# Expert stage in the order of the source, tokens gathered as float32 from x itself, 20 weight slots, last down-projection in two halves

## The chip, the cores and the metric

The program runs on one core of a Trainium2 chip. A core has five engines that run their own instruction streams and meet at semaphores: TensorE (PE, matrix multiply; its weight loads are listed apart as PEld), VectorE (DVE), ScalarE (ACT), GpSimd (POOL) and SyncE (SP, which here only issues DMAs). The metric is device time of one execution in microseconds (us), lower is better. Before the change the median of three runs is 1189.18 us (1188.09 to 1191.92).

## What is computed

Two transformer blocks on 256 tokens of width 1024, and a final RMS norm. The change lies in the last part of the second block, a mixture of 32 experts in 4 groups; every token goes to its two best experts:

```python
merged = sigmoid(gate_r) * ret_out + sigmoid(gate_d) * diff_out
x = x + g1 * dot(merged, w_out)
h2 = rmsnorm(x, norm_ffn) * (1.0 + sc2) + sh2
y = hierarchical_moe(h2, w_router_group, b_router_group, w_router_expert,
                     b_router_expert, w_exp_gate, w_exp_up, w_exp_down)
    # for a token and each of its two experts e, with the router's weight:
    # dot(silu(dot(h2, w_exp_gate[e])) * dot(h2, w_exp_up[e]), w_exp_down[e])
x = x + g2 * y
return rmsnorm(x, norm_final)
```

Each expert has 1024x512 gate and up matrices and a 512x1024 down matrix, all float32: 192 MB of weights for the stage.

## The kernel before

The stage (`moe`, from L1361) treats 32 experts as 16 pairs j, with 64 slots for tokens to an expert, so that a pair fills the 128 partitions. Its weights come as 192 loads of 1 MB (128 x 2048 floats) on SP's queue, in the order in which `stream` yields them: for each pair 4 loads of gate, 4 of down of the pair before, 4 of up. A load goes into the next of 18 slots in rotation: 4 of pool "early", 3 raw2h, 1 raw2, 2 raw2b, 4 raw, 1 raw2c, 3 spm. A slot's DMA waits until PE has read what lay there. SP is in order, so a DMA that waits holds back all behind it.

What PE does for a pair j, in the source's order:

- `up(j)` for the gate: 32 matmuls of 64 columns of tokens by 512 (L1442), two experts side by side; then tanh on ACT and a product on DVE;
- `down(j-1)`: 32 such matmuls (L1464) into two PSUM banks, which ACT and DVE split into a high and a low part (L1469, L1470);
- `up(j)` again for the up matrix;
- in every odd j but 7 and 15: `gather(j+1)`, which brings the tokens of the next two pairs into `xg` (L1407, 32 records of 128x256); call such a j a turn;
- `scatter(j-1)`: 8 matmuls with the transposed one-hot GT that add to Y, four PSUM banks (L1390, L1391);
- `slots_T(j+1)`: GT for the next pair (L1422, L1424), and `turned`: the hidden layer transposed by four matmuls whose stationary operand is `th[:, f:512:4]`, every fourth float (L1450).

For `gather`, the routing part ahead of the stage makes `xs`, x scaled by its norm and split into high and low halves, each regrouped so that 128 columns lie side by side (L1179 on ACT, L1182 on DVE, both for two token tiles). The gather multiplies `xs` with a one-hot G of the slots (L1398).

At j = 7 the stage drains and branches, for the case that an expert has more than 64 tokens; gather(8) comes right behind the branch. At j = 15 one more slot is taken for `nf` and `g2`, two row vectors that `rows` spreads over the partitions (32 matmul records, L872), and another for `yacc`, the sum of x and the experts. Then come down(14), the last scatter, and the last pair's down-projection in three pieces of columns (L1533 and `piece`), each followed by its product with g2, its own scatter (L1572, L1573, L1575), and its squares. The tail scales by the norm and writes out (L1548 to L1555).

A scheduler orders the instructions of each engine: the source's order is only its input, and matmuls of one helper can be put among those of another.

Of the kernel before, what the change touches and what calls it, by code (L numbers as in the profile page):

```python
# [25 lines left out]
NRAW = 4  # L26
CHECK = 7
NRAW2B = 2
# [4 lines left out]
PIECES = ((0, 512), (512, 256), (768, 256))  # L33
# [58 lines left out]
class Build:  # L92
# [135 lines left out]
    def sq_part(self, ss, x, t, half, n=512):  # L228

        scr = self.t(self.sm, [128, 512], "sqs", bufs=1)  # L230
        row = x[:, t, :] if len(x.shape) == 3 else x
        self.nc.scalar.activation(scr[:, 0:n], row[:, half * n:(half + 1) * n], AF.Square, accum_out=ss[:, t, half:half + 1])
# [39 lines left out]
    def setup(self):  # L272
# [8 lines left out]
        self.sp_ctx = ExitStack()  # L281
        self.sp = self.pool("sp", 3, ctx=self.sp_ctx, side="right")
# [655 lines left out]
    def block2(self, x, ss, inner, outer):  # L938
# [184 lines left out]
        xs = self.xs = [T(self.xtp, [128, 2, 8, 128], "xl", F32R) for _ in range(2)]  # L1123
# [48 lines left out]
        for t in range(2):  # L1172
# [16 lines left out]
    def moe_setup(self):  # L1189
# [11 lines left out]
        for i, v in enumerate((self.a2, self.sh2)):  # L1201
            w = T(p, [128, 8, 16], "spread")
            nc.vector.tensor_mul(w, v[:, :, None].to_broadcast([128, 8, 16]), cm[:, None, 228:244].to_broadcast([128, 8, 16]))
            nc.tensor.matmul(pp[:, i * 8:i * 8 + 8], w.rearrange("p a b -> p (a b)"), cm[:, 244:252], start=True, stop=True)
# [94 lines left out]
    def stream(self):  # L1299
# [29 lines left out]
        def down(j):  # L1329
            w2 = [d["w_exp_down_2"][0, e].rearrange("(p f) c -> p f c", f=4) for e in (2 * j, 2 * j + 1)]  # L1330
            if j < 15:
                for b in range(2):
                    for a in range(2):
                        raw = slot()
                        put(raw, w2[a][:, b * 2:b * 2 + 2, :])
                        yield raw
                return
            for c in range(2):
                raws = [slot() for _ in range(2)]
                for c0, w, i, f, nf in [z for z in LAST if z[0] // 512 == c]:  # L1340
                    if nf * w == 2048:
                        put(raws[i], w2[i][:, :, c0:c0 + w])
                    else:
                        o = raws[i][c0 // 256 % 2][:, f * w:(f + nf) * w]
                        nc.sync.dma_start(o.rearrange("p (f c) -> p f c", f=nf), w2[i][:, f:f + nf, c0:c0 + w])
                yield from raws

        for j in range(16):
            yield from wide("w_exp_gate_2", j)
            if j == 15:  # L1350
                yield slot()
            elif j not in (0, CHECK + 1):
                yield from down(j - 1)
            yield from wide("w_exp_up_2", j)
            if j == 15:
                yield slot()
                yield from down(14)
            if j in (CHECK, 15):
                yield from down(j)

    def moe(self, x, ctx):  # L1361
# [12 lines left out]
        slots += whole(self.raw, "raw", NRAW) + whole(self.raw2c, "raw2c", NRAW2C) + whole(self.sp, "spm", 3)  # L1374
# [18 lines left out]
        def gather(j):  # L1393

            G = []
            for t in range(2):
# [3 lines left out]
                G.append(o)  # L1400
            xg = xgs[0] = xgs[0] or T(self.xtp, [128, 8, 256], "xh")
# [12 lines left out]
            return G, xg  # L1414
# [64 lines left out]
        G, xg = gather(0)  # L1479
        hT = None  # L1480
        for j in range(16):
            pgt = up(j)
            if j == 0:
                self.weights()
                GT, ws = slots_T(0, G)
# [3 lines left out]
            if j == 15:  # L1489
# [3 lines left out]
            elif hT is not None:  # L1493
                down(hT)
            pu = up(j)
            nc.vector.scalar_tensor_tensor(th, th, ws, pu, op0=OP.mult, op1=OP.mult)  # L1496
            GTj = GT
            if j == 15:
                yacc = load()[0:2]
                last = []  # L1500
                down(hT, lambda: last.append(turned(th, p2, "xg")))
                scatter(14, GTp, yp[:, 0], yp[:, 1])
                for t in range(2):
                    for c in range(2):
                        ccs = slice(c * 512, (c + 1) * 512)
                        nc.vector.tensor_mul(yacc[t][:, ccs], Y[t][c], g2[:, ccs])  # L1506
                        nc.gpsimd.tensor_add(yacc[t][:, ccs], yacc[t][:, ccs], x[:, t, ccs])  # L1507
                break
            if j % 2 == 1 and j != CHECK:
                G, xg = gather(j + 1)  # L1510
# [6 lines left out]
            if j == CHECK:  # L1517
                drain(j)
                hT = None
                G, xg = gather(j + 1)  # L1520
                GT, ws = slots_T(j + 1, G)
        hTt = last[0]

        fs = T(p1, [128, 2, 4], "fss")
        yfs = T(self.xtp, [128, 8, 256], "xh").rearrange("p k s -> p (k s)")
        tail = ()
        for q, (c0, n) in enumerate(PIECES):
            if c0 % 512 == 0:
                raws = [load() for _ in range(2)]
            py = self.acc()  # L1530
            for f in range(4):
                for i in range(2):
                    nc.tensor.matmul(py[i * 64:(i + 1) * 64, 0:n], hTt[:, f, i * 64:(i + 1) * 64],  # L1533
                                     raws[i][(c0 // 256 % 2) if n == 256 else f // 2][:, f * n % 1024:f * n % 1024 + n], start=(f == 0), stop=(f == 3))
# [3 lines left out]
            tail = self.piece(q, c0, n, py, GTj, yacc, fs, nf, g2, yfs[:, c0:c0 + n])  # L1538
# [18 lines left out]
    def piece(self, q, c0, n, py, GT, yacc, fs, nf, g2, yf):  # L1557

        nc = self.nc
        T = self.t  # L1560
        cs = slice(c0, c0 + n)
        nc.vector.tensor_mul(yf, py[:, 0:n], g2[:, cs])
        if q == 0:
            yh, yl = T(self.sm, [128, 512], "pf", F32R), T(self.p2, [128, 512], "yl", F32R, 1)
            nc.scalar.copy(yh, yf)
            nc.vector.tensor_sub(yl, yf, yh.bitcast(F32))
        yield
        for t in range(2):
            pc = self.mis()
            g = GT[:, t * 128:(t + 1) * 128]  # L1570
            if q == 0:
                nc.tensor.matmul(pc, g, yh, start=True, stop=False)  # L1572
                nc.tensor.matmul(pc, g, yl, start=False, stop=True)  # L1573
            else:
                nc.tensor.matmul(pc[:, 0:n], g.bitcast(F32), yf, start=True, stop=True)  # L1575
            nc.vector.tensor_add(yacc[t][:, cs], yacc[t][:, cs], pc[:, 0:n])
            scr = T(self.sm, [128, 512], "sqs", bufs=1)
            nc.scalar.activation(scr[:, 0:n], yacc[t][:, cs], AF.Square, accum_out=fs[:, t, q:q + 1])
            if q == 0:
                nc.gpsimd.tensor_mul(yacc[t][:, cs], yacc[t][:, cs], nf[:, cs])  # L1580

    def overflow(self, p1, p2, x, Y):
# [5 lines left out]
        with tc.If(most > 64):  # L1588
            with tc.For_i(0, 32, 1) as e:
                n = nc.values_load(cnt[0:1, bass.ds(e, 1)], min_val=0, max_val=256)  # L1590
                with tc.If(n > 64):
# [5 lines left out]
                    def part(name, k):  # L1597
                        src = d[name][0, bass.ds(e, 1)]
                        src = src.rearrange("o (p f) c -> p (o f) c", f=4) if name == "w_exp_down_2" else src.rearrange("o (p k) c -> p (o k) c", k=8)
                        w = T(self.sm, [128, 512], "sqs", bufs=1)  # L1600
# [6 lines left out]
                    for b in range(1, 4):  # L1607
                        G, Gr = [], []
                        for t in range(2):
# [5 lines left out]
                            o = T(p2, [128, 64], f"Gr{t}", bufs=1)  # L1615
# [4 lines left out]
                        xg = T(p2, [128, 8, 64], "xg", bufs=1)  # L1620
# [107 lines left out]
```

## Time and profile before

| | us |
|---|---|
| median of three runs | 1189.18 |
| the profiled execution | 1188.83 |
| its span in the trace | 1186.9 |
| PE busy in the span | 1131.5 |
| first gate matmul of the expert stage, from the span's start | 723.4 |
| first gate matmul of pair 15 | 1136.6 |

The span is what the trace covers; 1.9 us of the execution lie outside it. A view by windows lists, for each stretch, its length, every engine's busy time with the number of records, the granted clock of PE (1.00 is the full 2.4 GHz level, 0.50 the 1.2 GHz one), the DMA engines' share and the rate. Timeline and chain rows begin with the start and the length of a run of like instructions. A float32 matmul over the full array appears as two records.

### The profile page before, as it was taken

What the parts mean: (1) busy time and instruction counts of PE and PEld (TensorE: products, weight loads), DVE (VectorE), ACT (ScalarE), POOL (GpSimd) and SP (SyncE); (2) the same over time, 40 slices, a digit from 0 to 9 for tenths busy, and PEclk for the clock granted to TensorE, in tenths of its full rate; (3) what the DMA queues carried; (4) which work ended last, traced back from release to release, by engine and by line L of the source; (5) the groups of instructions that cost most, each with busy time, mean ns of one, the idle gap of its engine ahead of it and who ended that gap; (6) DMA issues with size and microseconds to landing.
All of it is one profiled execution on the core that took longest, in us unless ns stands there. A gap on an engine that the chain in (4) does not pass through costs nothing. (4 is left out here: it accounts for less than half of the span.)

```text
span 1186.9 us, 16106 instructions
## 1 busy us (share of the span) xinstructions
PE 1131.5 (95%) x6502; PEld 808.6 (68%) x6503; DVE 550.8 (46%) x862; ACT 393.6 (33%) x679; POOL 188.6 (16%) x137
## 2 busy tenths in 40 slices
PE   7999988999999999999899999999999799999997
PEld 6788766898999798998899975434343344344443
DVE  2767655876666684788565643111111111111103
ACT  2434434555444445434544441111011011110112
POOL 0422531322011130532220210000000000000003
PEclk9999988999999999999999998999999999999999
DMA  8345524687777746657357575999999999999993
GB/s 269 105 144 177 178 87 142 245 279 288 248 283 255 244 142 194 197 162 264 142 152 285 182 281 218 421 421 419 421 421 421 420 420 420 421 421 421 421 415 129
DMA packets 86654, 331.64 MB, mean 279 GB/s; under 512 B 5520, under 2 KB 10272, under 8 KB 62512
## 3 DMA queue, kind: packets, MB, share of 16 engines
q1 hardware_dynamic: 84080, 327.70, 73.1%
q10 hardware_dynamic: 2448, 2.79, 0.8%
q8 instruction: 52, 0.85, 0.3%
q14 instruction: 26, 0.21, 0.0%
q0 software_dynamic: 48, 0.08, 0.0%
HBM read 329.50 MB, written 1.05 MB: 279 GB/s over the span
## 5 line engine op out<-in xcount | busy, mean ns | idle before, releaser
L145 DVE TENSOR_TENSOR lo<-raw,hi 128x1024 fp32r<-128x1024 f32 x156 | 208.0, 1342 | 96.2 <-ACT hi L144 95.8
L144 ACT CAST hi<-raw 128x1024 fp32r<-128x1024 f32 x176 | 183.6, 1047 | 203.2 <-PE acc L169 76.8
L169 PE MATMUL acc<-xl,hi 128*128 128x256 f32 x448 | 127.7, 285 | 0.9 <-DVE xl L958 0.8
L168 PE MATMUL acc<-xh,hi 128*128 128x256 f32 x448 | 128.0, 286 | 0.0
L170 PE MATMUL acc<-xh,lo 128*128 128x256 f32 x448 | 127.3, 284 | 0.0
L169 PEld LDWEIGHTS acc<-xl,hi 128*128 128x128 f32 x448 | 86.4, 193 | 1.4 <-DVE xl L958 1.3
L168 PEld LDWEIGHTS acc<-xh,hi 128*128 128x128 f32 x448 | 86.3, 193 | 0.1
L170 PEld LDWEIGHTS acc<-xh,lo 128*128 128x128 f32 x448 | 86.2, 192 | 0.1
L211 PE MATMUL acc<-hi,xh 128*128 128x512 f32 x208 | 84.2, 405 | 0.0
L212 PE MATMUL acc<-lo,xh 128*128 128x512 f32 x208 | 83.2, 400 | 0.0
L213 PE MATMUL acc<-hi,xl 128*128 128x512 f32 x208 | 82.3, 397 | 0.0
L1442 PE MATMUL mis<-raw,xh 128*64 128x512 f32 x288 | 79.5, 594 | 0.0
L1507 POOL TENSOR_TENSOR raw2h<-raw2h,x 128x512 f32<-128x512 f32 x4 | 5.0, 1280 | 458.1 <-DVE raw2h L1506 458.1
L169 PE MATMUL mis<-xl,hi 128*128 128x256 f32 x256 | 72.6, 284 | 1.4 <-DVE xl L270 1.4
L168 PE MATMUL mis<-xh,hi 128*128 128x256 f32 x256 | 72.7, 284 | 0.0
L170 PE MATMUL mis<-xh,lo 128*128 128x256 f32 x256 | 72.4, 283 | 0.0
L1488 DVE SCALAR_TENSOR_TENSOR pf<-pf,mis 128x512 f32<-128x512 f32 x16 | 11.0, 688 | 123.8 <-ACT pf L1487 123.7
L145 POOL TENSOR_TENSOR lo<-raw,hi 128x1024 fp32r<-128x1024 f32 x20 | 48.4, 2421 | 101.9 <-ACT hi L144 101.9
L1470 DVE TENSOR_TENSOR xh<-mis,xh 128x512 fp32r<-128x512 f32 x30 | 20.8, 692 | 88.4 <-ACT xh L1469 88.2
L856 DVE SCALAR_TENSOR_TENSOR ada<-raw,sc,ada 128x1024 f32<-128x1024 f32 x42 | 56.7, 1350 | 9.1 <-DMA raw<-in_w_ada 8.5
L1442 PE MATMUL mis<-spm,xh 128*64 128x512 f32 x200 | 58.0, 596 | 0.0
L1442 PE MATMUL mis<-raw2h,xh 128*64 128x512 f32 x200 | 57.6, 595 | 0.0
(464 smaller groups left out, 2133.8 us busy)
## 6 DMA issues: line engine op xcount, KB each, us to landing
raw<-in_w_in SPq DMA_DIRECT2D x46, 1024.0 KB, 5.4
raw<-in_w_ff SPq DMA_DIRECT2D x32, 1024.0 KB, 6.0
raw<-in_w_exp_up SPq DMA_DIRECT2D x25, 1024.0 KB, 19.8
raw<-in_w_ada SPq DMA_DIRECT2D x24, 1024.0 KB, 5.7
early<-in_w_exp_down SPq DMA_DIRECT2D x18, 1024.0 KB, 20.1
raw<-in_w_exp_down SPq DMA_DIRECT2D x17, 1024.0 KB, 19.8
raw2h<-in_w_exp_up SPq DMA_DIRECT2D x16, 1024.0 KB, 19.8
spm<-in_w_exp_gate SPq DMA_DIRECT2D x15, 1024.0 KB, 20.1
```

What stands on the lines that cost most here:

```text
L144: nc.scalar.copy(hi, raw)
L145: (nc.gpsimd if self.total in POOL else nc.vector).tensor_sub(lo, raw, hi.bitcast(F32))
L168: nc.tensor.matmul(o, hi[:, w], xh[:, k, :], start=(k == 0 and cb % 2 == 0), stop=False, skip_group_check=True)
L169: nc.tensor.matmul(o, hi[:, w], xl[:, k, :], start=False, stop=False, skip_group_check=True)
L170: nc.tensor.matmul(o, lo[:, w], xh[:, k, :], start=False, stop=(k == 7), skip_group_check=True)
L211: nc.tensor.matmul(o, xh[:, k, ts], hi, start=(k == k0), stop=False)
L212: nc.tensor.matmul(o, xh[:, k, ts], lo, start=False, stop=False)
L213: nc.tensor.matmul(o, xl[:, k, ts], hi, start=False, stop=(k == k1))
L856: nc.vector.scalar_tensor_tensor(a, raw[:, kk, :], self.sc[:, k:k + 1], a, op0=OP.mult, op1=OP.add)
L1442: nc.tensor.matmul(o[i * 64:(i + 1) * 64, :], xg[:, k, j % 2 * 128 + i * 64:j % 2 * 128 + (i + 1) * 64], raws[i][kk // 2][:, kk % 2 * 512: ...
L1470: nc.vector.tensor_sub(yp[:, 1, c, :], py[c], yp[:, 0, c, :].bitcast(F32))
L1488: nc.vector.scalar_tensor_tensor(th, th, 1.0, pgt, op0=OP.add, op1=OP.mult)
```

## The change

In the expert stage PE, DVE and ACT now run in the order of the source (`manual_schedule`); SP and POOL are still ordered by the scheduler. `gather` reads x itself as float32: the stationary operand is `x[:, t, k:1024:8]`, every eighth float, and the moving one is Gr, the one-hot times the norm's factor, made by eight short DVE operations (`scaled`). That is 16 float32 matmuls of 128x256. `xs` and its four operations are gone, and its two buffers ("xl") become slots 19 and 20. G is still made (`onehot`), for `slots_T`.

The order of loads at the end is new: gate 15, up 15, a slot for yacc, `last(0)` (columns 0 to 511 of the last pair's down matrices), down 14, `last(1)` (the other columns, in 5 DMAs). The slot for nf and g2, with its `rows`, moves from j = 15 to j = 13, just ahead of up(13). The first half of the last down-projection runs ahead of down(14) and goes into Y unscaled; the second half comes last in two pieces of 256 columns. POOL now does the second half's additions of x and the products with nf of the first half.

```diff
-            xk = x[:, t, :].rearrange("p (q k) -> p k q", k=8)
-            nc.scalar.mul(xs[0][:, t], xk, r)
...
-            nc.vector.scalar_tensor_tensor(xs[1][:, t], xk, r, xs[0][:, t].bitcast(F32), op0=OP.mult, op1=OP.subtract)
...
         for j in range(16):
             yield from wide("w_exp_gate_2", j)
-            if j == 15:
+            if j not in (0, CHECK + 1, 15):
+                yield from down(j - 1)
+            if j == 13:
                 yield slot()
-            elif j not in (0, CHECK + 1):
-                yield from down(j - 1)
             yield from wide("w_exp_up_2", j)
-            if j == 15:
-                yield slot()
-                yield from down(14)
-            if j in (CHECK, 15):
+            if j == CHECK:
                 yield from down(j)
+        yield slot()
+        yield from last(0)
+        yield from down(14)
+        yield from last(1)
...
+        slots += whole(self.raw, "raw", NRAW) + whole(self.raw2c, "raw2c", NRAW2C) + whole(self.xtp, "xl", 2) + whole(self.sp, "spm", 3)
...
+                    nc.vector.tensor_scalar(Gr[t][:, e * 64:(e + 1) * 64], iota, P[:, t, 2 * j + e:2 * j + e + 1], r3[:, t:t + 1],
+                                            op0=OP.is_equal, op1=OP.mult)
...
-                    for i, (part, t) in enumerate(((0, 0), (0, 1), (1, 0), (1, 1))):
-                        nc.tensor.matmul(ps[:, kk, :], self.xs[part][:, t, k, :], G[t], start=(i == 0), stop=(i == 3))
+                    for t in range(2):
+                        nc.tensor.matmul(ps[:, kk, :], x[:, t, k:1024:8], Gr[t], start=(t == 0), stop=(t == 1))
...
+        self.ordered = ctx.enter_context(self.tc.manual_schedule(engines=ORDERED))
...
+        yacc = load()[0:2]
+        hTt = turned(th, p2, "h15")
+        raws = [load() for _ in range(2)]
...
+        down(hT, first)
+        scatter(14, GTp, yp[:, 0], yp[:, 1])
+        for c in range(2):
+            ccs = slice(c * 512, (c + 1) * 512)
+            for t in range(2):
+                nc.vector.tensor_mul(yacc[t][:, ccs], Y[t][c], g2[:, ccs])
+                (nc.vector if c == 0 else nc.gpsimd).tensor_add(yacc[t][:, ccs], yacc[t][:, ccs], x[:, t, ccs])
...
+            nc.scalar.activation(yfs[:, 1024:1536], yacc[t][:, 0:512], AF.Square, accum_out=fs[:, t, 0:1])
+            nc.gpsimd.tensor_mul(yacc[t][:, 0:512], yacc[t][:, 0:512], nf[:, 0:512])
```

On PE, at the end of pair 4 (no gather there): before, from the last matmul of down on. "mis" are PSUM banks, "acc" the banks of Y, "xh" is xg in the rows of L1442 and the split result of down in those of L1390 and L1391.

```order
L1464 MATMUL mis_7157<-spm_7172,pf_7126 64x512
L1390 MATMUL acc_6546<-xh_6581,GT_6959 128x512
L1390 MATMUL acc_6548<-xh_6581,GT_6959 128x512
L1391 MATMUL acc_6546<-xh_6581,GT_6959 128x512
L1391 MATMUL acc_6548<-xh_6581,GT_6959 128x512
L1390 MATMUL acc_6547<-xh_6581,GT_6959 128x512
L1390 MATMUL acc_6549<-xh_6581,GT_6959 128x512
L1442 MATMUL mis_7186<-spm_7187,xh_6586 64x512
L1391 MATMUL acc_6547<-xh_6581,GT_6959 128x512
L1391 MATMUL acc_6549<-xh_6581,GT_6959 128x512
L1422 MATMUL mis_7220<-ca_84,G_1222_7055 128x128
```

After, at the same place of pair 4, from the last two matmuls of up on (lines L1454, L1389, L1390, L1434 are the old L1442, L1390, L1391, L1422):

```order
L1454 MATMUL mis_7168<-raw2c_7181,xh_6596 64x512
L1454 MATMUL mis_7168<-xl_7183,xh_6596 64x512
L1389 MATMUL acc_6544<-xh_6583,GT_6947 128x512
L1390 MATMUL acc_6544<-xh_6583,GT_6947 128x512
L1389 MATMUL acc_6546<-xh_6583,GT_6947 128x512
L1390 MATMUL acc_6546<-xh_6583,GT_6947 128x512
L1389 MATMUL acc_6545<-xh_6583,GT_6947 128x512
L1390 MATMUL acc_6545<-xh_6583,GT_6947 128x512
L1389 MATMUL acc_6547<-xh_6583,GT_6947 128x512
L1390 MATMUL acc_6547<-xh_6583,GT_6947 128x512
L1434 MATMUL mis_7202<-ca_87,G_1221_7027 128x128
```

The scatter and `slots_T` stood ahead of up, with one matmul of up among them; now all of up is ahead of the scatter.

On SP, the last loads of the stage before, from the last of gate 15 on (two DMAs of a half column range at L1316, then L1345); in brackets are the semaphores waited for, "PE_49" being PE's progress.

```order
L1316 DMA spm_9080<-in_w_exp_gate 128x2048 [waits DMAHW4_49,PE_49]
L1316 DMA early_9119<-in_w_exp_up 128x2048 [waits DMAHW5_49,PE_49]
L1316 DMA early_9121<-in_w_exp_up 128x2048 [waits DMAHW6_49,PE_49]
L1316 DMA early_9131<-in_w_exp_up 128x2048 [waits DMAHW7_49,PE_49]
L1316 DMA raw2h_9133<-in_w_exp_up 128x2048 [waits DMAHW0_49,PE_49]
L1316 DMA raw2h_9147<-in_w_exp_down 128x2048 [waits DMAHW1_49,PE_49]
L1316 DMA raw_1683_9149<-in_w_exp_down 128x2048 [waits DMAHW2_49,PE_49]
L1316 DMA raw2b_9166<-in_w_exp_down 128x2048 [waits DMAHW3_49,PE_49]
L1316 DMA raw2b_9168<-in_w_exp_down 128x2048 [waits DMAHW4_49,PE_49]
```

After, from the last load of gate 15 on:

```order
L1313 DMA early_8976<-in_w_exp_gate 128x2048 [waits DMAHW4_49,PE_49]
L1313 DMA early_8990<-in_w_exp_up 128x2048 [waits DMAHW5_49,PE_49]
L1313 DMA early_8992<-in_w_exp_up 128x2048 [waits DMAHW6_49,PE_49]
L1313 DMA early_9002<-in_w_exp_up 128x2048 [waits DMAHW7_49,DMAHW4_49,PE_49]
L1313 DMA raw2h_9004<-in_w_exp_up 128x2048 [waits DMAHW0_49]
L1313 DMA raw2h_9023<-in_w_exp_down 128x4x512 [waits DMAHW1_49]
L1313 DMA raw_1616_9024<-in_w_exp_down 128x4x512 [waits DMAHW2_49]
L1313 DMA raw2b_9042<-in_w_exp_down 128x2048 [waits DMAHW3_49]
L1313 DMA raw2b_9044<-in_w_exp_down 128x2048
L1313 DMA raw_9058<-in_w_exp_down 128x2048 [waits DMAHW5_49]
L1313 DMA raw_9060<-in_w_exp_down 128x2048 [waits DMAHW6_49]
L1343 DMA raw_9096<-in_w_exp_down 128x4x256 [waits DMAHW7_49]
```

The last load of gate 15 now stands in a buffer of "early". Of the four buffers of that pool one holds nf and g2 from j = 13 to the end, so that the third load of up 15 (early_9002) goes into the buffer in which that last load of gate 15 (early_8976) lies: it waits for that load's landing (DMAHW4) and for PE to have read it. The loads behind it wait for no PE.

## Rows read from the trace of the kernel before

**Rows 1.** The page's first part: busy time, share of the span, records.

```profile
PE 1131.5 (95%) x6502; PEld 808.6 (68%) x6503; DVE 550.8 (46%) x862; ACT 393.6 (33%) x679; POOL 188.6 (16%) x137
```

**Rows 2.** View by windows; pairs 0–14, 1, 2, 4, 5, 7–8, and 15 to the end.

```profile
core 0: us, PE busy (x) PEld busy (x) DVE busy (x) ACT busy (x) POOL busy (x), PEclk, DMA share, GB/s
723.40:1136.62 413.22, 399.38 (x1905) 174.41 (x1904) 66.84 (x135) 56.15 (x103) 0.00 (x0) 0.99 1.00 415
740.26:768.02 27.76, 27.76 (x148) 13.30 (x147) 5.66 (x11) 4.99 (x9) 0.00 (x0) 1.00 1.01 421
768.02:791.94 23.92, 23.92 (x116) 9.46 (x115) 3.82 (x9) 2.73 (x5) 0.00 (x0) 1.00 1.01 421
820.88:847.42 26.54, 25.70 (x115) 10.17 (x114) 4.05 (x10) 2.73 (x5) 0.00 (x0) 1.00 1.01 422
847.42:879.40 31.98, 31.05 (x148) 14.22 (x147) 5.31 (x10) 4.99 (x9) 0.00 (x0) 1.00 1.01 421
905.95:970.95 65.00, 56.66 (x262) 25.87 (x261) 9.24 (x19) 7.62 (x14) 0.00 (x0) 0.95 1.01 419
1136.62:1186.90 50.28, 42.25 (x201) 18.62 (x200) 12.62 (x25) 10.83 (x24) 9.17 (x9) 0.95 0.63 245
```

**Rows 3.** PE's waits from 717 on: us in total, times, longest.

```profile
PE mis L1407 <- DVE G L1398: 7.5, 2, 6.6
PE mis L1450 <- DVE pf L1496: 6.5, 9, 0.9
```

**Rows 4.** PE's timeline in pairs 1 and 2: start, length, what.

```profile
761.02 4.10 PE L1407 MATMUL mis<-G,xl 128*128 128x256 f32 x32
...
778.37 3.60 PE L1464 MATMUL mis<-raw2b,pf 128*64 128x512 f32 x16
781.80 7.04 PE L1442 MATMUL mis<-raw,xh 128*64 128x512 f32 x32
```

**Rows 5.** PE's timeline in pair 4, where up stands among the scatter.

```profile
836.60 1.07 PE L1442 MATMUL mis<-spm,xh 128*64 128x512 f32 x2
...
846.75 0.75 PE L1450 MATMUL mis<-ca,pf 128*128 128x128 f32 x4 [0.84 <-DVE pf L1496]
```

**Rows 6.** PE's timeline early in the first block: float32 matmuls of 128x256.

```profile
21.82 9.23 PE L183 MATMUL acc<-xf,raw 128*128 128x256 f32 x42
```

**Rows 7.** PEld's groups by line from 727 on: busy us, mean ns.

```profile
L1450 PEld LDWEIGHTS mis<-ca,pf 128*128 128x128 f32 x64 | 9.3, 216 | 13.6 <-DVE pf L1496 9.7 <-ACT xh L1413 3.6 <-issue 0.3
...
L1422 PEld LDWEIGHTS mis<-ca,G 128*128 128x128 f32 x32 | 4.3, 142 | 3.2 <-issue 1.6
```

**Rows 8.** DVE's timeline in the routing.

```profile
706.42 2.08 DVE L1182 SCALAR_TENSOR_TENSOR xl<-x,r,xl 128x1024 fp32r<-128x1024 f32 x1 [0.82 <-ACT xl L1179]
...
711.77 2.06 DVE L1182 SCALAR_TENSOR_TENSOR xl<-x,r,xl 128x1024 fp32r<-128x1024 f32 x1 [0.36 <-ACT xl L1179]
...
717.22 0.75 DVE L1398 TENSOR_TENSOR G<-cm,P 128x256 fp32r<-128x256 f32 x2
```

**Rows 9.** View by windows: gather(0), its slow part, and gather(8).

```profile
717.70:723.40 5.70, 5.70 (x34) 5.57 (x34) 2.75 (x8) 1.41 (x3) 0.00 (x0) 0.66 0.00 0
717.70:721.50 3.80, 3.80 (x18) 3.80 (x19) 1.67 (x6) 0.56 (x1) 0.00 (x0) 0.50 0.00 0
...
948.70:954.95 6.25, 6.25 (x34) 6.25 (x35) 1.80 (x4) 1.46 (x3) 0.00 (x0) 0.61 1.02 417
```

**Rows 10.** Loads of 1 MB into an idle queue, us to landing (last).

```profile
raw<-in_w_ret_o SPq DMA_DIRECT2D x4, 1024.0 KB, 5.3
```

**Rows 11.** The chain that ended last, in order of time: start, length.

```profile
1137.69 1.76 PE mis L872 x14
...
1177.78 0.44 DVE xh L1562
```

**Rows 12.** DVE's groups by line in the tail: busy us, mean ns.

```profile
L1506 DVE TENSOR_TENSOR raw2h<-acc,early 128x512 f32<-128x512 f32 x4 | 2.6, 684 | 0.1
```

**Rows 13.** The page's costliest groups: a POOL operation of 128x512 in the tail.

```profile
L1507 POOL TENSOR_TENSOR raw2h<-raw2h,x 128x512 f32<-128x512 f32 x4 | 5.0, 1280 | 458.1 <-DVE raw2h L1506 458.1
```

More of the change, by code (lines that the diff above doesn't have):

```diff
@@ L1329, in down @@
         def down(j):
[L1330 to L1346, printed above, removed]
+            for b in range(2):
+                for e in (2 * j, 2 * j + 1):
+                    raw = slot()
+                    put(raw, d["w_exp_down_2"][0, e].rearrange("(p f) c -> p f c", f=4)[:, b * 2:b * 2 + 2, :])
+                    yield raw
@@ new lines, in last @@
+        def last(c):
+            raws = [slot() for _ in range(2)]
+            for c0, w, i, f, nf in [z for z in LAST if z[0] // 512 == c]:
+                w2 = d["w_exp_down_2"][0, 30 + i].rearrange("(p f) c -> p f c", f=4)
+                if nf * w == 2048:
+                    put(raws[i], w2[:, :, c0:c0 + w])
+                else:
+                    o = raws[i][c0 // 256 % 2][:, f * w:(f + nf) * w]
+                    nc.sync.dma_start(o.rearrange("p (f c) -> p f c", f=nf), w2[:, f:f + nf, c0:c0 + w])
+            yield from raws
@@ L1477, in drain @@
             self.overflow(p1, p2, x, Y)
-        G, xg = gather(0)
+        self.ordered = ctx.enter_context(self.tc.manual_schedule(engines=ORDERED))
+        xg = gather(scaled(0))
+        self.scratch = xg.rearrange("p k s -> p (k s)")
+        self.weights()
+        G = onehot(0)
         hT = None
@@ L1488, in moe @@
             nc.vector.scalar_tensor_tensor(th, th, 1.0, pgt, op0=OP.add, op1=OP.mult)
-            if j == 15:
+            if hT is not None and j < 15:
+                down(hT)
+            if j == 13:
                 nf, g2 = load()[0:2]
@@ L1492, in moe @@
                 self.rows(self.col("nfin", 0, 8), nf, self.mis)
-            elif hT is not None:
-                down(hT)
+            turn = j % 2 == 1 and j not in (CHECK, 15)
+            if turn:
+                Gr = scaled(j + 1)
+                G = onehot(j + 1)
             pu = up(j)
+            if j == 0:
+                GT, ws = slots_T(0, G)
             nc.vector.scalar_tensor_tensor(th, th, ws, pu, op0=OP.mult, op1=OP.mult)
@@ L1498, in moe @@
             if j == 15:
[L1499 to L1507, printed above, removed]
                 break
-            if j % 2 == 1 and j != CHECK:
-                G, xg = gather(j + 1)
+            if turn:
+                xg = gather(Gr)
             if hT is not None:
@@ L1519, in moe @@
                 hT = None
-                G, xg = gather(j + 1)
+                xg = gather(scaled(j + 1))
+                G = onehot(j + 1)
                 GT, ws = slots_T(j + 1, G)
-        hTt = last[0]
-        fs = T(p1, [128, 2, 4], "fss")
-        yfs = T(self.xtp, [128, 8, 256], "xh").rearrange("p k s -> p (k s)")
+        yacc = load()[0:2]
+        hTt = turned(th, p2, "h15")
+        raws = [load() for _ in range(2)]
+        py = self.mis()
+        for f in range(4):
+            for i in range(2):
+                nc.tensor.matmul(py[i * 64:(i + 1) * 64, :], hTt[:, f, i * 64:(i + 1) * 64], raws[i][f // 2][:, f * 512 % 1024:f * 512 % 1024 + 512],
+                                 start=(f == 0), stop=(f == 3))
@@ L1526, in moe @@
+        fs = T(p1, [128, 2, 4], "fss")
+        yfs = T(self.xtp, [128, 2048], "xh")
+        for t in range(2):
+            nc.scalar.activation(yfs[:, 1024:1536], yacc[t][:, 0:512], AF.Square, accum_out=fs[:, t, 0:1])
+            nc.gpsimd.tensor_mul(yacc[t][:, 0:512], yacc[t][:, 0:512], nf[:, 0:512])
+        raws = [load() for _ in range(2)]
         tail = ()
[L1527 to L1530, printed above, removed]
+        for q in range(2):
+            c0 = 512 + 256 * q
+            py = self.mis()
```

68 lines of the change are left out of this document (33 added, 35 removed).

## The prediction

> **What bounds the kernel now.** I read the page's busy shares first, then the expert stage by windows, then PE's waits, and the timeline of single pairs. PE is busy for 95% of the span [rows 1], so PE's own time is the first thing to count. But the stage has a second engine at its limit: from 723.4 to 1136.6 us the DMA share is 1.00 at 415 GB/s, 421 in every pair [rows 2], which is 1.049 MB in 2.49 us. Both run beside each other without PE waiting for weights: the waits of any size on PE's side are for one-hots and for the product ahead of `turned` [rows 3]. So inside the stage a microsecond taken from PE counts, as long as the loads stay ahead. The pairs differ: a pair without a gather takes 23.92 us in the source's order (pair 2) and 26.54 in the scheduler's interleaved order (pair 4) [rows 2]. The reason is visible: matmuls of 64 columns run two side by side, 32 of them in 7.0 us or 16 in 3.6 [rows 4], while a lone pair of them among a scatter takes 1.07 [rows 5], and when up ends with nothing behind it, PE stands 0.84 us for the product on DVE [rows 5]. Turns likewise: 27.76 plain, 31.98 interleaved [rows 2].
>
> **The change part by part.** The sum is made against the profiled execution: 723.4 to the first gate, 413.2 for pairs 0 to 14, 50.3 from gate 15 to the end, 1.9 outside the span: 1188.8. That is 0.35 below the median, which I add back at the end.
>
> *The gather.* Before, 32 records take about 3.94 us at full clock (4.10 less the overhang of the last) [rows 4]. After, 16 float32 matmuls of 128x256 are 32 records too, but of the kind of L183: 42 of them in 9.23 us, less an overhang of 0.38 of the last, is 0.216 each [rows 6], so a gather takes 6.91 us, 2.97 more. This holds if loading every eighth float as weights hides behind the record ahead of it. The trace has no step of eight. The nearest rows are `turned`'s loads with a step of four: mean 216 ns against 142 for the like transposes of packed columns [rows 7], so a step is not free. The bounds are nothing (the load overlaps the record ahead, whose 0.216 us it just fits) and 0.074 us for each of 32 records in 8 gathers, 19 us. I take nothing: four loads and transposes of L1450 end 0.75 us after their start [rows 5], under 0.19 each, so consecutive loads do overlap.
>
> The Trainium skill speaks against the strided read here: "SBUF — State Buffer", section "Specifications (TRN2)", says that memory lines are 16 bytes and that full bandwidth needs at least two hits in a line; a step of eight floats has one. Its rule gives no figure for the loss. By that rule a step of four floats has one hit too, so the trace agrees as far as rows 7 go, and the sum by it is the rival below.
>
> *Up to gate 0.* The two DVE splits in the routing, 2.08 and 2.06 us, fall away, and what follows them in DVE's order (the choice of the second token tile, P, G) comes about 4.1 earlier [rows 8]. Eight short DVE operations make Gr where two made G in 0.75: about +0.4. gather(0) ran 3.8 us at a granted clock of 0.50 and took 5.70 in all [rows 9], so the low clock cost 1.8; I take the same loss, 6.91 + 1.8 = 8.7, +3.0. The counting matmuls of `weights()` only change sides. Sum: -4.1 + 0.4 + 3.0 = -0.7. Bounds: -2.5 if the clock is full there, +1.1 if the slow part is twice as long. All 20 slots have been loaded by then; SP waits for nothing new ahead of the first freed slot.
>
> *Pairs 0 to 14.* Pair 0 keeps its 16.9 (723.40 to 740.26). Six turns of 27.76 - 3.94 + 6.91 = 30.73 make 184.4. Six pairs without a gather (2, 4, 6, 10, 12, 14) at 23.92 make 143.5 [rows 2]. Pairs 7 and 8 with drain, branch and gather(8) take 65.0 now [rows 2]. gather(8) takes 6.25 there at a mean clock of 0.61 [rows 9], 2.3 more than at full clock; after, 6.91 + 2.3 = 9.2, +3.0; half of what interleaving costs a pair, 26.54 - 23.92, goes, -1.3; so 66.7. `rows` moves here from pair 15: 14 of its 32 records take 1.76 us [rows 11], all of them 4.0 at most; they no longer break pairs, 3.5. Sum: 16.9 + 184.4 + 143.5 + 66.7 + 3.5 = 415.0, against 413.2: **+1.8**. The order gives back about 14.6 (2.6 or 4.2 in most pairs), the float32 gather takes 18 and more.
>
> *The new wait on SP.* The nf/g2 slot, taken at j = 13, holds one of the four "early" buffers for good, and so the third load of up 15 waits until PE has read the last load of gate 15. SP is in order: the fourth load of up 15, both of `last(0)`, four of down 14 and `last(1)` queue behind it, about 10 MB. The loads before it come in by the time the stream has moved 162 MB: 20 loads lie there before gate 0, the first slot frees 3.6 us into gate 0 [rows 4], the first load lands 5.3 later [rows 10], and 161 x 2.49 = 401 more, so 410 us after gate 0. Gate 15 begins at 415 and ends at 422. DMA is idle for 12 to 15 us, and PE then waits for it. With g the start of gate 15: the blocked load is issued at g + 7.05. Into an idle queue a load takes 5.3 us [rows 10], the next seven 2.49 each: the last load of down 14 lands at g + 7.05 + 5.3 + 17.4 = g + 29.75. PE has done up 15, `turned`, the first half of the last down and half of down 14 by then (3.6 us after each pair of loads, the last at g + 28.5). Half of down 14 remains, 3.6 [rows 4]: its end E is g + 33.4.
>
> *The tail.* After E: the last copies and the first two matmuls of the scatter, about 1.7; product and sum on DVE, 0.68 each [rows 12]; a square on ACT, taken as 0.7 like these; then POOL, whose four operations alternate between products and sums, 1.28 each, 5.1 [rows 13]; then an addition of 256 columns, 0.44. That is E + 9.3. Only then comes the second piece's product with g2, which now stands at 1177.78 [rows 11], 9.1 before the end of the span. So the end is E + 18.4 = g + 51.8, against 50.28 [rows 2]: **+1.5**. What `rows` no longer costs here, and the tail that runs earlier, are used up by the wait for the loads. The bounds are -5.4 (no wait: PE runs gate, up, `turned`, `last(0)`, down 14 through in 26.5 us, and the end is g + 44.9) and +1.5 more (later landings).
>
> *Free edits.* onehot(j+1) and Gr run on DVE, which is busy 4 to 6 us of a pair's 24 to 28 [rows 2]; if that cover failed, PE would wait at the gather. Two more slots let the loads run 5 us further ahead; as PE did not wait for weights before, they bring nothing except at the end, where the wait undoes it.
>
> Total: -0.7 + 1.8 + 1.5 = **+2.6**, 1191.4 for an execution like the profiled one, and 1191.8 beside the median.
>
> **The rivals.** *A: no stall in the last pair.* If the reload does not hold back PE, because the loads behind it get done in time, the end is g + 44.9 and the last term -5.4 in place of +1.5: -0.7 + 1.8 - 5.4 = -4.3, 1184.9, faster. For it: loads of 1 MB need only 2.49 us each, and the first half of up 15 is still to be done when the wait ends. Against: 10 MB need 25 us, and gate 15 is nearly the last work with weights at hand. *B: strided weights cost time.* From 0.216 us for the load on, each excess counts 256 times. With the difference between rows 7 in full, +19, 1211; with a tenth of a record (0.022), +5.6, 1197.4. Slower than before. For it: the step of four already takes half as long again; against: the float32 record has twice the length of those transposes to hide it. The rule on 16-byte lines, of the Trainium skill's page "SBUF — State Buffer", is of this kind. *C: the fixed order makes PE wait for DVE or ACT in each turn*, since nothing can be put into the gap between up and `turned`, or before the gate that reads a fresh xg. One wait like the 0.84 [rows 5] in each of 14 pairs is +11.8, 1203.6; in the six turns alone +5, 1196.8. For it: the gather's last banks are evacuated only as the scatter starts; against: the plain pairs 1 and 2 have that same order, and PE's busy time there is the whole window [rows 2]. *D: the order does not change pairs 4, 5 and the like*: excluded by the program's order, and not counted.
>
> **How the numbers follow.** About 0.3% (3.6 us) is what a measurement of this kernel can tell from no change: faster is below 1185.6, slower above 1192.75. The forecast gets 0.70; with its bounds (gate 0 by 1.8 either way, landings, the branch) it runs from 1188 to 1195, 0.02 of it faster, 0.48 the same, 0.20 slower. A gets 0.08, of which 0.06 is faster. B gets 0.10 and C 0.08, slower. The remaining 0.04 are split: 0.02 faster, 0.02 slower. Sums: faster 0.10, the same 0.50, slower 0.40. For 8 in 10 the range is 1187 to 1199: below lies A, above most of B and half of C.
>
> **What would show it.** In the profile after: the gathers' 32 records in 6.9 us with load records that do not set the pace (else B); pairs 2, 4, 6 all at 23.9 and turns at 30.7 (else C); gate 0 near 722.7 and gate 15 near 1137.7; a hole of some 13 us in the DMA share around gate 15, then PE waiting for early's load in up 15 and for each pair of loads to down 14 (else A); and four POOL operations that end just before the last addition. The prediction is wrong if one of the three sums is off by more than 3 us.

## The result, and the profile after

The changed kernel takes 1200.9 us (1197.54 to 1203.73, five runs), the kernel before 1189.72 beside it (five runs): a ratio of 1.0087, 95% interval 1.0061 to 1.0113. It is slower by about 0.9%, where 1191.8 and a range of 1187 to 1199 were predicted. With the repeat below, nine executions have a median of 1200.2. The profiled one took 1197.54, with a span of 1195.9. In what follows, gate 0 and gate 15 are the first gate matmuls of pairs 0 and 15.

PE's busy share is the one of [rows 1], with 7 us more in it:

```profile
PE 1138.9 (95%) x6502; PEld 827.5 (69%) x6503; DVE 560.1 (47%) x923; ACT 389.4 (33%) x677; POOL 184.6 (15%) x135
```

By windows, to be laid beside [rows 2] (length, busy time of each engine, granted clock, DMA share, rate): pairs 0 to 14, pair 1 (a turn), pair 2, pairs 7 and 8, pair 13, pair 15 to the end, and gather(0).

```profile
721.00:1143.44 422.44, 412.89 (x1934) 198.09 (x1933) 81.48 (x207) 58.54 (x108) 0.00 (x0) 0.99 0.97 403
738.07:769.75 31.68, 31.68 (x147) 17.21 (x146) 7.44 (x18) 4.99 (x9) 0.00 (x0) 1.00 1.01 420
769.75:793.67 23.92, 23.92 (x115) 9.46 (x114) 3.18 (x7) 2.73 (x5) 0.00 (x0) 1.00 1.01 420
904.89:972.69 67.80, 59.38 (x261) 28.05 (x261) 11.23 (x28) 7.72 (x14) 0.00 (x0) 0.92 1.01 420
1083.91:1119.51 35.60, 35.60 (x179) 20.77 (x178) 7.75 (x21) 7.33 (x13) 0.00 (x0) 1.00 1.01 420
1143.44:1195.90 52.46, 37.37 (x169) 15.13 (x168) 11.86 (x26) 8.46 (x20) 6.54 (x7) 0.94 0.59 221
712.66:720.54 7.88, 7.88 (x32) 7.86 (x33) 1.79 (x4) 1.69 (x3) 0.00 (x0) 1.00 0.64 266
```

Three terms give the difference between the two profiled executions, 9.0 us of span. Gate 0 comes at 721.0 in place of 723.4, -2.4 (0.6 of it ahead of the change: a router matmul in front of all the edits, L1145, starts at 703.25 in place of 703.81). Pairs 0 to 14 take 422.4 in place of 413.2, +9.2. Pair 15 to the end takes 52.5 in place of 50.3, +2.2. A pair without a gather is now 23.92, as the source's order was to give. The loss is in the turns: 31.68 where 27.76 stood and 30.73 was predicted. PE is busy throughout a turn, so nothing waits there; the gather is longer. Its row in the timeline, against the first of [rows 4], and the first row of the scatter behind it:

```profile
758.82 8.05 PE L1419 MATMUL mis<-Gr,x 128*128 128x256 f32 x32
...
766.51 0.58 PE L1389 MATMUL acc<-xh,GT 128*128 128x512 f32 x1
```

From its start to that of the scatter are 7.70 us, 0.2405 a record, where [rows 6] gave 0.216.

The reload that waits for gate 15 is there, as the DMA share in the 14.5 us before 1150.5 shows (0.00), and so is PE's wait for it. The stream runs dry near 1132.5, 18 us ahead of the reload's issue. The three parts are the view by windows around gate 15, SP's waits from 1130 on, and PE's from 1100 on (us in total, times, longest):

```profile
1132.00:1133.00 1.00, 1.00 (x8) 0.42 (x6) 0.00 (x0) 0.29 (x1) 0.00 (x0) 1.00 0.10 41
1136.00:1150.50 14.50, 14.50 (x74) 6.33 (x72) 1.06 (x3) 0.96 (x2) 0.00 (x0) 1.00 0.00 1
1150.50:1156.00 5.50, 3.95 (x20) 1.05 (x14) 0.69 (x1) 0.60 (x1) 0.00 (x0) 1.00 0.80 286
```

```profile
SPq L1313 <- PE mis L1454: 22.1, 1, 22.1
```

```profile
PE mis L1454 <- DMA early<-in_w_exp_up: 1.6, 1, 1.6
PE mis L1454 <- DMA raw2h<-in_w_exp_up: 1.4, 1, 1.4
```

The end of the chain that ended last (start, length) runs from the blocked load over the stream of the last weights to POOL's four operations in turn:

```profile
1150.57 0.33 SPq L1313
...
1150.94 7.03 DMA raw2h<-in_w_exp_up
1157.99 3.01 SPq L1343
...
1161.05 16.82 DMA raw<-in_w_exp_down
...
1180.66 1.57 POOL raw2h L1562
1182.24 1.23 POOL raw2h L1557
1183.47 1.23 POOL raw2h L1562
1184.70 1.23 POOL raw2h L1557
...
1185.95 0.42 DVE raw2h L1604
```

### The profile page after: what moved, and what is told of

Read it like the earlier page. It is cut to its first block, busy times and chain, and to the rows that moved or that the text cites. A ratio compares the mean times of both kernels' runs of the same rounds, so it can differ in the third digit from the quotient of the medians.

```text
span 1195.9 us, 16148 instructions
## 1 busy us (share of the span) xinstructions
PE 1138.9 (95%) x6502; PEld 827.5 (69%) x6503; DVE 560.1 (47%) x923; ACT 389.4 (33%) x677; POOL 184.6 (15%) x135
## 5 line engine op out<-in xcount | busy, mean ns | idle before, releaser
L1562 POOL TENSOR_TENSOR raw2h<-raw2h,early 128x512 f32<-128x512 f32 x2 | 2.8, 1420 | 473.7 <-ACT xh L1561 473.7
L1419 PE MATMUL mis<-Gr,x 128*128 128x256 f32 x256 | 66.8, 421 | 8.2 <-PEq L1613 6.2
L1419 PEld LDWEIGHTS mis<-Gr,x 128*128 128x128 f32 x256 | 63.4, 337 | 14.7 <-PEq L1613 6.6
L1454 PE MATMUL mis<-early,xh 128*64 128x512 f32 x248 | 60.4, 595 | 1.6 <-DMA early<-in_w_exp_up 1.6
L1454 PE MATMUL mis<-raw,xh 128*64 128x512 f32 x216 | 61.3, 593 | 0.0
```

The lines of the kernel that those rows point to most:

```text
L1419: nc.tensor.matmul(ps[:, kk, :], x[:, t, k:1024:8], Gr[t], start=(t == 0), stop=(t == 1))
L1454: nc.tensor.matmul(o[i * 64:(i + 1) * 64, :], xg[:, k, j % 2 * 128 + i * 64:j % 2 * 128 + (i + 1) * 64], raws[i][kk // 2][:, kk % 2 * 512: ...
```

## The experiments

All are compared with the kernel before on the same chip, and with the 1200.2 of the changed kernel's nine executions. The kernel before has medians of 1189.7 to 1190.8 in the series beside them, so about 1 us of a difference to 1200.2 can be the series'. Theory: the step of eight floats slows the gather's weight loads. Rivals: the float32 form itself; the reload that waits; the fixed order.

### The changed kernel again

> The changed kernel once more. In its profile each record of a gather takes 0.241 us and no stretch of the routing runs at a granted clock of 0.50 (gate 0 at 721.0 us), but that execution is the quickest of five (1197.5; median 1200.9). Theory: the other executions have a stretch at 0.50 around the first gather, which makes gate 0 some 2 to 4 us later. Expected: 1198 to 1204, gathers at 0.241 again; if this profile shows a stretch at 0.50 in the routing, gate 0 at 723 to 725. Rival: the spread sits in the wait for the last loads, then gate 0 is the same and the end of the stage moves.

1199.43 (1197.34 to 1200.73), 1.0068 of before (1.0045 to 1.009). The gathers are at 0.2405 again. Two windows, gather(0) and the first gate of pair 1, show stretches of a granted clock at 0.50 that the first profile did not have (mean 0.83 and 0.80); a third lies in PE's wait for the loads of up 15 (0.76 from 1158 to 1165):

```profile
713.67:722.77 9.10, 9.10 (x32) 8.56 (x33) 1.79 (x4) 1.70 (x3) 0.00 (x0) 0.83 0.54 225
740.29:748.91 8.62, 8.62 (x34) 2.76 (x34) 0.00 (x0) 0.59 (x1) 0.00 (x0) 0.80 1.01 421
```

The first two cost 1.2 and 1.7 us (7.88 and 6.92 in the first profile). Gate 0 is at 723.2, as expected, and the rival has no support: pair 15 to the end takes 52.7. A further source of spread lies ahead of the change: in the eleven profiles of the changed kernel and its variants, whose matmuls run in the same order up to there, that router matmul (L1145 or L1146) starts between 701.5 (`e2_steps`) and 708.8 us (`e5_scheduler`), here at 704.3. So the 1197.54 was a lucky execution of the changed kernel.

### Packed weights for the gather

```diff
-nc.tensor.matmul(ps[:, kk, :], x[:, t, k:1024:8], Gr[t], ...)
+nc.tensor.matmul(ps[:, kk, :], x[:, t, k * 128:(k + 1) * 128], Gr[t], ...)
```

> The gather's weights are read as 128 floats side by side, x[:, t, 128k:128k+128], in place of every eighth float; nothing else is changed, so other columns of x are gathered than the reference's. Theory (the step of eight floats slows the weight loads): records at 0.216 in place of 0.241 us, 0.8 us less for each gather, 8 gathers and their low-clock part: 6 to 8 us less than the changed kernel, about 1193 to 1195. Rival (a float32 matmul in this place takes 0.241 whatever it reads, by its moving operand or PSUM): no change.

1194.21 (1191.46 to 1195.71), 1.0027 of before (1.0015 to 1.0039), 6.0 less than the changed kernel. The gather of pair 1 in the timeline, and its weight loads (busy us, mean ns), first here and then in the changed kernel:

```profile
759.87 7.17 PE L1419 MATMUL mis<-Gr,x 128*128 128x256 f32 x32
...
L1419 PEld LDWEIGHTS mis<-Gr,x 128*128 128x128 f32 x32 | 6.0, 190 | 1.6 <-issue 0.8
...
L1419 PEld LDWEIGHTS mis<-Gr,x 128*128 128x128 f32 x32 | 7.8, 337 | 0.8 <-issue 0.8
```

It is 6.82 us to the scatter, 0.2132 a record, and 7.70 with the step of eight; a load takes 0.190 us in place of 0.337. Pairs 0 to 14 take 416.3 (to the first gate matmul of pair 15 at 1138.38), 6.1 less. Only the floats of x that are read as weights differ, so the theory holds and its size too; a float32 matmul at this place costs what [rows 6] showed.

### Other steps

```diff
+steps = [8, 1, 2, 3, 4, 5, 6, 7]
...
-x[:, t, k:1024:8]
+x[:, t, k:k + 127 * step + 1:step]
```

> Gather number 0 reads weights with a step of 8 floats, the next seven with steps of 1, 2, 3, 4, 5, 6 and 7 (so other columns of x than the reference's). Theory (each float from a line of 16 bytes of its own costs): 0.216 at step 1, little more at 2, the full 0.241 from step 4 on. Rival 1 (the loss grows with the step): a steady rise to step 8, 0.22 at 4. Rival 2 (only steps of 32 bytes meet the same bank): odd steps and step 4 at 0.216, step 8 alone at 0.241.

One execution, 1191.98. The timeline's rows of the gathers with steps 1, 2, 3, (4 behind the branch,) 5, 6 and 7, and the loads at steps 3 and 5:

```profile
757.04 7.17 PE L1423 MATMUL mis<-Gr,x 128*128 128x256 f32 x32
811.79 7.18 PE L1423 MATMUL mis<-Gr,x 128*128 128x256 f32 x32
866.55 7.24 PE L1423 MATMUL mis<-Gr,x 128*128 128x256 f32 x32
...
988.63 7.48 PE L1423 MATMUL mis<-Gr,x 128*128 128x256 f32 x32
1043.69 7.54 PE L1423 MATMUL mis<-Gr,x 128*128 128x256 f32 x32
1102.72 7.78 PE L1423 MATMUL mis<-Gr,x 128*128 128x256 f32 x32
...
L1423 PEld LDWEIGHTS mis<-Gr,x 128*128 128x128 f32 x31 | 6.7, 252 | 0.8 <-issue 0.8
...
L1423 PEld LDWEIGHTS mis<-Gr,x 128*128 128x128 f32 x32 | 7.2, 307 | 0.8 <-issue 0.8
```

Lengths include an overhang of the last record of some 0.35; the pace to the next group is 0.2132, 0.2135, 0.2153, 0.2229, 0.2245 and 0.2322 us for steps 1, 2, 3, 5, 6 and 7. The loads take 0.190, 0.196, 0.252, 0.307, 0.310 and 0.325 us there, and the pace moves little up to the load of 0.252. At the step behind the branch part of the gather ran at the low clock, so that its pace is taken from the next run. The theory, flat from 4 on, falls, since 5 and 6 are well below 8; so does rival 2, since 7 is not at 0.216. Rival 1, a steady rise, seems to fit but lacks step 4. The next run supplies it and asks whether the cost goes on rising.

```diff
+steps = [8, 4, 12, 16, 1, 8, 10, 14]
+x.rearrange("p t d -> p (t d)")[:, k:k + 127 * step + 1:step]
```

> As e2_steps, over both token tiles in one row so that steps up to 16 floats fit (other values than the reference's are gathered): gather 0 at step 8, then 4, 12, 16, the one behind the branch at 1, then 8, 10, 14. If the cost grows with the step without end: 0.218 to 0.220 a record at 4, 0.241 at 8, about 0.26 at 12, 0.28 at 16. If it is only the number of floats read from one line, it stays at 0.241 from 8 on. If a step of 64 bytes meets one bank: a jump at 16 above all the others.

One execution, 1203.02. The rows with steps 4, 12, 16, and then, after one more of step 8, 10 and 14, and the load at step 4:

```profile
765.39 7.84 PE L1423 MATMUL mis<-Gr,x 128*128 128x256 f32 x32
820.80 8.96 PE L1423 MATMUL mis<-Gr,x 128*128 128x256 f32 x32
877.33 7.47 PE L1423 MATMUL mis<-Gr,x 128*128 128x256 f32 x32
...
1054.18 7.66 PE L1423 MATMUL mis<-Gr,x 128*128 128x256 f32 x32
1113.33 8.16 PE L1423 MATMUL mis<-Gr,x 128*128 128x256 f32 x32
...
L1423 PEld LDWEIGHTS mis<-Gr,x 128*128 128x128 f32 x32 | 7.5, 329 | 0.8 <-issue 0.8
```

That is 0.2341, 0.2690 and 0.2225, then 0.2405 (step 8), 0.2283 and 0.2439 a record, with loads of 0.329, 0.370, 0.306, 0.337, 0.318 and 0.341 us. All three expectations fail, and with them rival 1 of the run above: 4 is dearer than 5 or 6, 12 is the dearest, 16 no dearer than 5. That a step costs is shown, and how much for each (most from a single gather); so is that pace and load go up and down together once the load is 0.306 us or longer. By what rule a step makes a load long, these runs leave open.

### The held slot left out of the rotation

```diff
+if held and n % len(self.slots) == held[0]:
+    n += 1
...
-yield slot()
+raw = slot()
+held.append((n - 1) % len(self.slots))
+yield raw
```

> After the slot for nf and g2 is taken at j = 13, the rotation leaves that slot out, so the third load of up 15 goes to the next buffer and waits for a reader that is long done. Theory (one reload that waits for gate 15 stalls the stream): the DMA hole around gate 15 goes, PE runs through up 15, the first half of the last down and down 14, and the end comes 6 to 7 us earlier, about 1194. Rival (the tail is bound by POOL's four operations and by the arrival of the last loads in any case): less than 3 us.

1195.48 (1192.36 to 1198.46), 1.0044 of before (1.0023 to 1.0064): 4.7 less than the changed kernel. By windows, pair 15 to the end takes 47.76, and the stream runs on in the place of the hole:

```profile
1145.14:1192.90 47.76, 35.72 (x169) 14.37 (x168) 11.86 (x26) 8.46 (x20) 6.54 (x7) 0.90 0.36 136
1136.00:1150.00 14.00, 14.00 (x72) 6.11 (x69) 1.67 (x4) 0.96 (x2) 0.00 (x0) 1.00 1.03 409
```

The reload costs 4.7 in the profile and in the medians, less than the 6 to 7 expected: with it gone, PE still waits for DVE and ACT around `turned`, and needs 28.0 us from gate 15 to the end of down 14, not 26.5 (33.5 with the reload).

### Without the fixed order

```diff
-self.ordered = ctx.enter_context(self.tc.manual_schedule(engines=ORDERED))
```

> The changed kernel without the fixed order on PE, DVE and ACT; all else stays. Theory (the fixed order saves what broken pairs of matmuls cost): pairs without a gather at 26.5 and turns at 36 us in place of 23.9 and 31.7 in most of the stage, 12 to 16 us more, about 1212 to 1215. Rival (the order as such is worth little here): within 3 us of 1200.

1234.81 (1231.36 to 1237.61), 1.0365 of before (1.0334 to 1.0395): 34.6 more than the changed kernel, more than twice what was expected. Gate 0 is 4 to 7 us later in its profile, most of it ahead of the change (the router matmul above), and pairs 0 to 14 take 455.15, 32.7 more. The timeline of a turn shows the gather cut into pieces by up, and lone pairs of 1.07 as in [rows 5]:

```profile
874.08 1.07 PE L1454 MATMUL mis<-raw2h,xh 128*64 128x512 f32 x2
875.08 2.76 PE L1419 MATMUL mis<-Gr,x 128*128 128x256 f32 x10
877.78 3.65 PE L1454 MATMUL mis<-raw2h,xh 128*64 128x512 f32 x14
881.36 1.33 PE L1419 MATMUL mis<-Gr,x 128*128 128x256 f32 x4
```

The fixed order is worth more here than in the old pairs, where the trace before has 21.3 us over the source's order: four pairs at 26.55 for 23.92, two turns at 31.97 and two at 28.94 for 27.75. The prediction's 14.6, near which the expectation lay, does not follow from its rows. Pairs 6, 10, 12 and 14 have the old 26.55 again; turns 5, 9 and 11 are at 35.3 for 31.7, and pair 13 with its `rows` at 43.4 for 35.6. Why the turns lose more than before is not shown; the old gather was broken too, in four of six turns.

### Where the stream of weights is the floor

The old gather (xs, 18 slots) in the changed kernel, with the held slot left out:

```diff
-nc.tensor.matmul(ps[:, kk, :], x[:, t, k:1024:8], Gr[t], ...)
+for i, (part, t) in enumerate(((0, 0), (0, 1), (1, 0), (1, 1))):
+    nc.tensor.matmul(ps[:, kk, :], self.xs[part][:, t, k, :], Gr[t], ...)
```

> The changed kernel with the gather of before (xs split in the routing, 32 records of packed weights, 18 slots), in the source's order, and with the slot of nf and g2 left out of the rotation, so it is e3_skip with the old gather. If PE alone sets the time: 8 x 3.8 = 30 less for the gathers, 4 more in the routing, 1195.5 - 26 = about 1169. If the stream of weights is the floor (174 MB at 2.49 us from the first freed slot at about 727, the last landing at 1166 to 1168, and 18 to 20 us of tail behind it): 1185 to 1189, with PE waiting for loads in the last pairs.

1188.63 (1186.61 to 1191.42), 0.999 of before (0.9975 to 1.0005). PE alone would give 1169. In the chain that ended last PE is no longer the bulk of the stage's end; loads of 20 us hang one behind another, and PE's waits from 900 on name loads:

```profile
1086.78 19.89 DMA raw2h<-in_w_exp_gate
...
1106.73 19.82 DMA raw2c<-in_w_exp_up
...
1126.62 21.15 DMA raw2h<-in_w_exp_up
```

```profile
PE mis L1463 <- DMA raw<-in_w_exp_up: 3.7, 3, 1.3
```

And the kernel before with nothing but the fixed order:

```diff
+self.ordered = ctx.enter_context(self.tc.manual_schedule(engines=ORDERED))
 G, xg = gather(0)
```

> The kernel before with nothing changed but the fixed order of PE, DVE and ACT in the expert stage. If the order is worth what broken pairs cost on PE: 14 us less up to gate 15. But the DMA share is 1.00 all through the stage of before and its last load lands at 1167.5, 19 us before the end: then PE waits for weights at the end and the time falls by 0 to 4 only, 1186 to 1190. Rival (PE alone): about 1176.

1189.16 (1187.73 to 1192.62), 0.9992 of before (0.9974 to 1.001). Again PE waits for weights, which it did not in [rows 3]:

```profile
PE mis L1408 <- DVE G L1399: 14.8, 8, 6.3
...
PE mis L1443 <- DMA early<-in_w_exp_up: 2.6, 2, 1.3
PE mis L1443 <- DMA spm<-in_w_exp_up: 1.3, 1, 1.3
```

The fixed order also makes PE wait for the one-hot ahead of each gather, 14.8 us where [rows 3] has 7.5, so this run alone would not tell the stream from that wait; but PE still runs into the loads of the last pairs, and the run above, without that wait in its turns, does too. Both say the same: with 18 slots the stage cannot end much earlier however quick PE is. The last packet of weights ends 443.6 us after gate 0 before the change, 443.8 in the first of these runs, 441.3 with the 19 slots of the next section and 439.0 with 20 and the held slot left out. So a slot brings the end of the stream forward by about 2.4 us; no run changes the number of slots alone.

### Versions that beat both

x copied once in float32 with every eighth float side by side (19 slots), the held slot left out, and slots_T(0) ahead of the first up:

```diff
+self.xk = T(self.xtp, [128, 2, 8, 128], "xl")
...
+nc.scalar.copy(self.xk[:, t], x[:, t, :].rearrange("p (q k) -> p k q", k=8))
...
-nc.tensor.matmul(ps[:, kk, :], x[:, t, k:1024:8], Gr[t], ...)
+nc.tensor.matmul(ps[:, kk, :], self.xk[:, t, k, :], Gr[t], ...)
```

> The changed kernel with three edits: x is copied once in float32 with every eighth float side by side (two ACT operations in the routing, one buffer, so 19 slots) and the gather reads the copy; the slot held by nf and g2 is left out of the rotation; slots_T(0) stands ahead of the first up. The result is the reference's. Theory: 0.87 us less for each of 8 gathers (7), 4.7 less from the end of the stage as in e3_skip, 1 to 3 less where PE stands in pair 0: 1200 - 13 = 1186 to 1188, and faster than the kernel before by 2 to 4. Rival (with PE faster, the stream of weights becomes the limit): not under 1192.

1186.73 (1183.59 to 1189.5), 0.9973 of before (0.9959 to 0.9987): 13.5 less than the changed kernel, of which 6 and 4.7 are measured apart above; the rest is not separated. The gather is at 0.2132 with the reference's columns, as it was with the other columns of `e1_packed`. The third edit alone:

```diff
-pu = up(j)
 if j == 0:
     GT, ws = slots_T(0, G)
+pu = up(j)
```

> The changed kernel with one move: slots_T(0) ahead of the first up in place of behind it. Theory (behind up, PE stands 1.1 us for the chain from slots_T over DVE to turned in pair 0, and in some executions a stretch at a granted clock of 0.50 follows in pair 1, which cost 1.7 us in the repeat of the changed kernel): 1 to 2.5 us less, 1197.5 to 1199, no stretch at 0.50 near 740 us. Rival (the wait is only moved): the same as the changed kernel, 1200.

1198.37 (1195.29 to 1199.71), 1.0062 of before (1.0039 to 1.0084). Its profile has no stretch at 0.50 in pair 1, and PE's wait in pair 0 is 0.2 in place of 1.1. In the fixed order with `slots_T(0)` behind up, three of six profiles have that stretch (`again`, `e3_skip`, `e10_steps16`); with it ahead, none of three. The 1.8 us less are within the spread of the medians, so this part is supported and not settled. Last, the best version with POOL in the source's order too:

```diff
-ORDERED = {PE, DVE, Activation}
+ORDERED = {PE, DVE, Activation, Pool}
```

> e4_packed_copy with POOL in the source's order too, so that in the tail both additions of x come before both products with nf (the scheduler had them in turn: product, sum, product, sum). Theory (the last addition waits for all four POOL operations, 5.3 us in e3_skip): the second sum ends some 2 us earlier and the end with it, 1184 to 1185.5, faster than before by 5. Rival (the chain behind the second piece is bound by its weights or by DVE): within 0.7 of e4_packed_copy, 1186.7.

1186.45 (1183.7 to 1188.01), 0.9966 of before (0.9952 to 0.9979). POOL's timeline has the two sums first, the last of them done at 1173.75, 2.0 us after DVE's last product, and POOL is no longer in the chain ahead of the last piece; without the order the last sum came fourth and 5.3 us after POOL's first (the last row is `e4_packed_copy`'s):

```profile
1171.26 2.49 POOL L1564 TENSOR_TENSOR xl<-xl,x 128x512 f32<-128x512 f32 x2 [460.61 <-DVE xl L1563]
1173.71 2.49 POOL L1569 TENSOR_TENSOR xl<-xl,raw2b 128x512 f32<-128x512 f32 x2
...
1173.70 1.25 POOL L1564 TENSOR_TENSOR xl<-xl,x 128x512 f32<-128x512 f32 x1
```

From gate 15 to the end this profile has 45.4 us and e4_packed_copy's 46.9, 1.6 less; the medians differ by 0.3 only. The gain of the order on POOL is seen in the trace and not in the times.

## Why the prediction was wrong, step by step

**The gather** is the step that failed: "I take nothing" for the strided weights, a price put at nothing. The bounds stood there, nothing and 0.074 us a record; the truth was 0.027 (0.2405 against 0.2132), 7 us in 8 gathers, and 6.0 in the medians. The argument was that four transposes with a step of four end in 0.75 us, so that loads overlap. Overlap was true and not enough: loads of 0.190 to 0.252 us leave the pace at 0.213 to 0.215, and the one of 0.337 at step eight makes it 0.2405. Nor was `turned` a fair proxy: at its step of four a load took 0.216 [rows 7], and the same step in the gather made it 0.329 and cost 0.021 a record. The rule of the Trainium skill ("SBUF — State Buffer", section "Specifications (TRN2)"), that fewer than two hits in a 16-byte line lose bandwidth, named the right suspect, and the trace agrees as to the loss at eight. By it steps of 4 to 16, one hit each, should cost alike, and they go from 0.2225 to 0.2690: here the measurement decides. Rival B, "a tenth of a record (0.022)", 1197.4, was the case that came, at a chance of 0.10 that was too low for a step with a price in the nearest row.

**Pairs 0 to 14** were 422.4 against 415.0. Six turns at 31.68 for 30.73 are 5.7 of it: 0.79 each is the gather, the other 0.16 stands at the scatter behind it. Pairs 7 and 8 are 1.1 more, `rows` in pair 13 0.4 (3.9 for 3.5), pair 0 0.2. Pairs without a gather were right to the hundredth. Of the three sums only this one is off by more than the 3 us that the prediction set as its sign of being wrong. Its sentence that the order gives back 14.6 is a slip beside the sum: the pairs give 21.3, and 415.0 is worked out with them. Behind the branch two errors met: from the start of gather(8) to the next matmul it took 11.6 us, not 9.2 (1.1 of it PE's wait for the one-hot G), and the rest of the two pairs 1.2 less than forecast.

**Gate 0** was predicted at 722.7, and was at 721.0 and 723.2: inside the bounds. It moves with the clock in gather(0) and with what lies ahead of the stage. Counted from the router matmul it comes after 19.6 us before, 19.0 in the repeat, whose gather(0) has the low clock too (-0.6, forecast -0.7), and 17.7 in the first profile at the full clock.

**The new wait and the tail** were right: the load issued 7.1 us into gate 15 (7.05), PE at work on it 4.9 later (5.3), down 14 done at gate 15 + 33.5 (33.4), the end 18.9 behind it (18.4), by the mechanism named. The DMA hole was 18 us and not 12 to 15, as gate 15 came 7 us later behind a stream that ended when forecast (411 us after gate 0 for 410). The price of the alternative was off: without the wait 47.8 from gate 15 to the end and not 44.9. Of the 2.9 stand 1.5 ahead of the end of down 14 (28.0 for 26.5, with PE's waits of 0.9 and 0.7 around `turned`) and 1.3 behind it (19.7 for 18.4).

**Rival C** did not come in the changed kernel: the plain turns have no wait. In the old kernel the same order did bring such waits, for the one-hot (`e7_before_ordered`). **Rival A** was refuted by the hole and by PE's waits of 1.6 and 1.4 us for the loads behind it.

**From profile to median.** The prediction carried the 0.35 us between the profile before and its median over to after, where it is 3.4. The repeat's profiled execution, 1200.73, is close to the median, and its span is 3.2 longer than the first: 1.0 ahead of the change, 1.2 in gather(0) and 1.7 in pair 1 at the low clock, 0.3 from gate 15 on, and 1.0 less in pairs 7 and 8 (66.8 for 67.8). Low clock in gather(0) is nothing new, as [rows 9] have it; that in pair 1 is, and it stands behind a wait of 1.1 in pair 0 that the fixed order brought. Of the 9.1 us by which the forecast missed, 6.1 stand in the profiled execution (7.4 in pairs 0 to 14, 0.7 at the end, -1.7 up to gate 0, -0.3 outside the span), and 3.0 are such differences between executions.

## What to carry to other kernels

Before reading a matmul's weights with a step, measure that step in that form of matmul: here loads of up to 0.252 us were hidden and loads of 0.306 us and more set the pace, and then every record pays. A buffer held to the end in a rotation moves one reload behind the wrong reader, and a queue in order makes a stall of it; look for loads that wait for a reader later than their neighbours do. Where DMA share is 1.00 beside a busy PE, see when the stream would end by itself: in the two runs with 18 slots time taken from PE bought nothing, because the last loads came no earlier after gate 0.

## What was not expected of the hardware

The cost of a step in weight loads is no simple function of it: 0.2132, 0.2135, 0.2153, 0.2341, 0.2229, 0.2245, 0.2322, 0.2405 us a record for steps 1 to 8 floats, then 0.2283 at 10, 0.2690 at 12, 0.2439 at 14 and 0.2225 at 16. And a part of the program that no edit touches took between 701.5 and 708.8 us up to the same matmul, so that differences under some 2 us need many executions.
